# Where the expert tokens' norm weight, scale and shift are applied: on token rows or on turned blocks

## The chip, the cores and the metric

The kernel runs on one core of one Trainium2 chip. The metric is device time in microseconds (us); the kernel before was run three times with a median of 1957.68 us (1955.96 to 1957.83). TensorE does matmuls and transposes (a transpose is a matmul with an identity), VectorE and ScalarE the elementwise work, GpSimd indirect DMAs and small work, SyncE issues the weight loads. Each engine works through its own instructions in program order and waits on semaphores for the others.

## The reference, cut to what matters

The program is a transformer block with a mixture of experts, and a second block behind it. The part that the change touches, with one batch row, 1024 tokens of 1024 channels, 16 experts of 128 tokens each:

```python
x = x + ga1 * branch_merge(px, h_mx, w_fourier, w_mlstm, w_out)
hx2 = modulate(rmsnorm(x, g_norm2), sh2, sc2)       # x * rstd * g * (1 + sc2) + sh2
# expert_choice(hx2, ...)
aff  = softmax(hx2 @ w_router)                      # 1024 x 16
vals, idx = top_k(aff.T, 128)                       # each expert takes 128 tokens
xs   = hx2[idx]                                     # 16 x 128 x 1024
hid  = silu(xs @ w_gate[e]) * (xs @ w_up[e])
y    = (hid @ w_down[e]) * vals
x = x + ga2 * zeros.at[idx].add(y)
```

Products are done to float32 accuracy: each operand is split into a high and a low part, and three matmuls (high·high, high·low, low·high) stand for one.

## The kernel before, in words

`mods` holds the modulation rows in device memory: row 0 is ga1, row 1 sh2, row 2 the norm weight times (1 + sc2), called A2, row 3 ga2. `router` loads rows 2 and 1 a second time as columns, one number per partition and block of 128 channels, into `ash`.

*Output projection and router* (`out_proj`, L1397). Eight tiles of 128 tokens. While TensorE does tile t+1, lanes of small steps that a planner deals out by its own costs do the norm, the routing (`route`, L1521) and the sort of tile t. `route` computes the affinities `aff`, and turns x into the modulated row h2 = x·rstd·A2 + sh2: for tiles 0 to 6 with two VectorE operations over 128x1024, for tile 7 with one on ScalarE and two on GpSimd (L1554 on). h2 and its affinities go to device memory as `h2d`. The sort of the affinities (`top`, `join`) runs on VectorE: maxima by eights of each pair of tiles, and many small merge steps (`tk`). Behind the loop the memory product of the second block (`memory`, L1480; a key and a value half, buffers `memr`, `kvm`) is taken half by half where `next(self.mem)` stands.

*Experts* (`experts`, L1626). From the sorted lists a count matrix `cm` is built; `index(e)` gets the 128 token numbers of an expert with two matmuls, and `gather(e)` fetches their rows from `h2d` into `xs`. `transp` turns four blocks of 128x128 into one PSUM bank `pa`: ScalarE copies it, rounded, into the high half of `xT`, and VectorE subtracts that from the bank into the low half. `prod` is one product: eight steps k, each of six matmuls, with weights split by ScalarE (high) and VectorE (low) from `raw` into `w` ahead of use (`prefetch`). A transposition for a later product is put in behind steps 2 and 4 (`turned`). The order per expert: the up product of expert e, in which expert e+1's rows are turned; g·pu on VectorE (in place, in the spare columns of `xs`); the gate product of expert e+1, in which g is turned into `hT`; the down product of expert e; the weighting and the scatter-add. In the code as traced all instructions carry the line of a recording helper, L67; the names of the tiles tell them apart.

In `experts` before the first expert, the order is: two gathers, the value half of `memory`, the first splits (`prefetch`), then the turning of expert 0's rows.

Of the kernel before, what the change touches and what calls it, by code (L numbers as in the profile page):

```python
# [9 lines left out]
FT = mybir.dt.float32  # L10
# [3 lines left out]
AF = mybir.ActivationFunctionType  # L14
OP = mybir.AluOpType
# [10 lines left out]
NE = 16  # L26
# [126 lines left out]
class Kern:  # L153
# [1235 lines left out]
    def load_rows(self):  # L1389
        nc = self.nc  # L1390
        self.rr = r1, r2 = self.slot(FT, "r1"), self.slot(FT, "r2")
        self.rows = ga1, A2, sh2 = r1.t[:, 0:1024], r1.t[:, 1024:2048], r2.t[:, 0:1024]
        self.AT = r2.t[0:48, 1024:2048]
        for i, v in ((0, ga1), (2, A2), (1, sh2)):
            nc.scalar.dma_start(v, self.bcast(self.mods[i:i + 1], 1024))

    def out_proj(self):  # L1397

# [102 lines left out]
    def post(self, n, ps, x, h2, hT, t):  # L1501

        nc = self.nc
        sm = self.sm[:, (t % 2) * 32:(t % 2) * 32 + 32]
        c = slice(n * 512, (n + 1) * 512)
        self.soon(ps)
        nc.vector.tensor_mul(h2[:, c], ps, self.rows[0][:, c])
        nc.vector.tensor_add(x[:, c], x[:, c], h2[:, c])
        nc.scalar.activation(h2[:, c], x[:, c], AF.Square, accum_out=sm[:, n:n + 1])
        yield  # L1510
        yield 1.0
        yield from self.until(x[:, c])
        p = self.bank("pa", (4, 128))
        for k in range(4):
            nc.tensor.transpose(p[:, k], x[:, (4 * n + k) * 128:(4 * n + k + 1) * 128], self.idn)
        nc.scalar.activation(hT[:, 4 * n:4 * n + 4], p, AF.Copy)
        yield 0.6
        if n:
            self.spawn(self.route(t, x, h2, hT), 2)

    def route(self, t, x, h2, hT):  # L1521

        nc = self.nc
        g = nc.gpsimd
        sm = self.sm[:, (t % 2) * 32:(t % 2) * 32 + 32]
        _, A2, sh2 = self.rows
        nc.sync.dma_start(self.x1d[t * 128:(t + 1) * 128], x)
        yield 0.6
        yield from self.until(hT)
        p = self.bank("pa")  # L1530
        for k in range(8):
            nc.tensor.matmul(p[0:16, 0:128], self.wr[:, k], hT[:, k], start=(k == 0), stop=(k == 7))
        lg = self.tk.t[0:16, 1920:2048]
        if t < 7:
            nc.scalar.activation(lg, p[0:16, 0:128], AF.Copy)
        else:
            self.soon(p[0:16, 0:128])
            nc.vector.tensor_copy(lg, p[0:16, 0:128])
        g.tensor_add(sm[:, 2:3], sm[:, 0:1], sm[:, 1:2])
        self.inv_sqrt(sm[:, 3:4], sm[:, 2:3], 1.0 / D, EPS)  # L1540
        yield 0.6
        yield from self.until(lg)
        p = self.bank("pa")
        nc.tensor.transpose(p[:, 0:16], lg, self.idn[0:16, 0:16])
        z = sm[:, 8:24]
        self.soon(p[:, 0:16], sm[:, 3:4])
        nc.vector.scalar_tensor_tensor(z, p[:, 0:16], sm[:, 3:4], self.shw, op0=OP.mult, op1=OP.add)
        nc.vector.tensor_reduce(sm[:, 4:5], z, axis=AX.X, op=OP.max, negate=True)
        nc.scalar.activation(z, z, AF.Exp, bias=sm[:, 4:5], accum_out=sm[:, 5:6])
        self.soon(sm[:, 5:6])  # L1550
        nc.vector.reciprocal(sm[:, 5:6], sm[:, 5:6])
        nc.vector.tensor_scalar(self.aff[:, :, 0:16], z[:, None, :].to_broadcast([128, 2, 16]), sm[:, 5:6], None,
                                op0=OP.mult)
        if t < 7:  # L1554
            nc.vector.scalar_tensor_tensor(h2[:, 0:1024], x, sm[:, 3:4], A2, op0=OP.mult, op1=OP.mult)
            nc.vector.tensor_add(h2[:, 0:1024], h2[:, 0:1024], sh2)
        else:
            nc.scalar.activation(h2[:, 0:1024], x, AF.Copy, scale=sm[:, 3:4])
            g.tensor_mul(h2[:, 0:1024], h2[:, 0:1024], A2)
            g.tensor_add(h2[:, 0:1024], h2[:, 0:1024], sh2)  # L1560
        g.tensor_copy(h2[:, 1024:1040], self.aff[:, 0, 0:16])
        g.dma_start(self.h2d[t * 128:(t + 1) * 128], h2)
        yield 0.6
        yield from self.until(self.aff)
        p = self.bank("pa")
        nc.tensor.transpose(p[0:64, 0:128], self.aff.rearrange("p a b -> p (a b)"), self.idn)
        nc.scalar.activation(self.AT[:, t * 128:(t + 1) * 128], p[0:48, 0:128], AF.Copy)

        w = self.tk.t[0:48]
        at = 768 + 128 * (t // 2) if t < 6 else 1536  # L1570
        new = w[:, 1408:1536]
        q = 32 * (t % 2)
        nc.scalar.activation(w[q:q + 16, at:at + 128], p[q:q + 16, 0:128], AF.Copy)
        if t % 2:
            self.spawn(self.top(w[:, at:at + 128], w[:, 1280:1408] if t == 1 else new, 0), 1)
            if t > 1:
                self.spawn(self.join(new), 1)
        self.routed += 1
        yield 0.5
# [46 lines left out]
    def experts(self, r2):  # L1626
        nc = self.nc
# [26 lines left out]
        xs = {}  # L1654
# [17 lines left out]
                                         in_offset=bass.IndirectOffsetOnAxis(ap=self.idx[:, e:e + 1], axis=0))  # L1672
            xs[e] = s

        def transp(src, o, k4):

            hi, lo = (o.t[:, i * 1024:(i + 1) * 1024] for i in range(2))
            p = self.bank("pa", (4, 128))
            for k in range(4):
                kk = k4 * 4 + k  # L1680
                nc.tensor.transpose(p[:, k], src[:, kk * 128:(kk + 1) * 128], self.idn)
            pf = p.rearrange("p a b -> p (a b)")
            c = slice(k4 * 512, (k4 + 1) * 512)
            nc.scalar.activation(hi[:, c], pf, AF.Copy)
            nc.vector.tensor_sub(lo[:, c], pf, hi[:, c].bitcast(FT))

        def prod(o, between=None):

# [9 lines left out]
                    between(k)  # L1698
            return pss

        def turned(src, dst, key):

            def between(k):
                if k == 2:
                    dst[key] = self.slot(FR, "xT")
                if k in (2, 4):
                    transp(src, dst[key], k // 2 - 1)
            return between

        def silu(e, pss):  # L1710
            s = xs[e].t[:, 1040:2064]
            for n in range(2):
                nc.scalar.activation(s[:, n * 512:(n + 1) * 512], pss[n], AF.Silu)
            return s

        for e in range(2):
            index(e)
            gather(e)
        next(self.mem)
        self.spare, self.ahead = 4, 3  # L1720
        self.prefetch()
        for _ in self.mem:
            pass
        xT, hT = {0: self.slot(FR, "xT")}, {}
        for k4 in range(2):
            transp(xs[0].t, xT[0], k4)
        index(2)
        self.spare, self.ahead, self.raw_max = 1, 5, 20
        self.prefetch()
# [3 lines left out]
        for e in range(NE):  # L1733
            if e == NE - 1:
# [1 line left out]
                nc.gpsimd.dma_start(ir.t[:, 0:1024], self.bcast(self.I["iota"], 1024))  # L1736
                nc.gpsimd.tensor_scalar(io.t[:, 0:1024], ir.t[:, 0:1024], self.last, None, op0=OP.is_equal)
                self.free(ir)
            pu = prod(xT[e], turned(xs[e + 1].t, xT, e + 1) if e + 1 < NE else None)
            self.free(xT.pop(e))  # L1740
            for n in range(2):
                c = slice(n * 512, (n + 1) * 512)
# [1 line left out]
            if e + 1 < NE:  # L1744
                if e + 2 < NE:
                    gather(e + 2)
                g[e + 1] = silu(e + 1, prod(xT[e + 1], turned(g[e], hT, e)))
            if e == NE - 1:
                hT[e] = self.slot(FR, "xT")
                for k4 in range(2):  # L1750
# [572 lines left out]
```

## Time and profile before

| quantity | value |
|---|---|
| median of 3 runs | 1957.68 us (1955.96 to 1957.83) |
| profiled execution, its own time | 1955.41 us |
| its span | 1953.6 us |
| TensorE, busy | 1871.4 us |
| VectorE, busy | 1417.4 us |
| ScalarE, busy | 872.1 us |
| GpSimd, busy | 161.2 us |
| granted TensorE clock, mean | 0.985 |

The profile comes from one execution; its span is the stretch that the hardware profiler covers, and the time of the execution is 1.8 us more. Busy time of an engine says nothing on whether it is waited for: that is read from timelines and from the waits of a stage. The granted clock is in parts of TensorE's full speed. The experts take about a third of the span.

### The profile page before, as it was taken

What the parts mean: (1) busy time and instruction counts of PE and PEld (TensorE: products, weight loads), DVE (VectorE), ACT (ScalarE), POOL (GpSimd) and SP (SyncE); (2) the same over time, 40 slices, a digit from 0 to 9 for tenths busy, and PEclk for the clock granted to TensorE, in tenths of its full rate; (3) what the DMA queues carried; (4) which work ended last, traced back from release to release, by engine and by line L of the source; (5) the groups of instructions that cost most, each with busy time, mean ns of one, the idle gap of its engine ahead of it and who ended that gap; (6) DMA issues with size and microseconds to landing.
All of it is one profiled execution on the core that took longest, in us unless ns stands there. A gap on an engine that the chain in (4) does not pass through costs nothing.

```text
span 1953.6 us, 23920 instructions
## 1 busy us (share of the span) xinstructions
PE 1871.4 (96%) x9226; PEld 1511.7 (77%) x9226; DVE 1417.4 (73%) x2129; ACT 872.1 (45%) x1243; POOL 161.2 (8%) x162
## 2 busy tenths in 40 slices
PE   6899999999999999959999999999989999999997
PEld 3687888888877787748888888888868977678786
DVE  7797675555653645689999999999973977663554
ACT  6623432322322332227777777777854223342300
POOL 1300000000000002110111001010030000000011
PEclk9999999999999999979999999999999999999999
DMA  8100125433313533478999999999951110011312
GB/s 354 65 27 14 54 87 216 172 142 130 119 69 148 173 129 135 166 311 314 378 381 381 382 395 395 400 392 387 365 183 43 34 43 22 28 45 44 129 65 76
DMA packets 64541, 361.02 MB, mean 185 GB/s; under 512 B 9742, under 2 KB 10775, under 8 KB 30380
## 3 DMA queue, kind: packets, MB, share of 16 engines
q1 hardware_dynamic: 50652, 319.22, 42.1%
q0 software_dynamic: 9680, 34.37, 5.7%
q10 hardware_dynamic: 4096, 5.91, 0.9%
q8 instruction: 72, 1.18, 0.2%
q14 instruction: 41, 0.34, 0.0%
HBM read 329.96 MB, written 29.52 MB: 184 GB/s over the span
## 4 chain that ended last, share of the span: by engine, by line
PE 89%; DVE 6%; ACT 2%; DMA 1%; issue 1%; POOL 0%; ACTq 0%; POOLq 0%; DVEq 0%; SPq 0%
PE pm L67 78%; PE pa L67 11%; DVE tk L67 1%; DVE gt L67 1%; DVE w L67 1%; DMA bd<-gd 1%; DVE mw L67 0%; DMA b<-yd 0%; DMA wgr<-in_w_g 0%; DVE tm L67 0%; ACT gt L67 0%; ACT x L67 0%; DVE b L67 0%; ACT w L67 0%; POOL stat L67 0%
## 5 line engine op out<-in xcount | busy, mean ns | idle before, releaser
L67 DVE TENSOR_TENSOR w<-raw,w 128x1024 fp32r<-128x1024 f32 (+1 forms) x500 | 586.9, 1217 | 89.6 <-ACT w L67 85.2
L67 PE MATMUL pm<-w,xT 128*128 128x512 f32 x2304 | 552.7, 397 | 3.0 <-ACT xT L67 2.5
L67 ACT ACTIVATE w<-raw 128x1024 fp32r<-128x1024 f32 (+1 forms) x500 | 507.5, 1052 | 104.9 <-PE pm L67 101.0
L67 PEld LDWEIGHTS pm<-w,xT 128*128 128x128 f32 x2304 | 429.9, 189 | 99.1 <-ACT xT L67 3.1
L67 PE MATMUL pm<-hT,w 128*128 128x512 f32 x1536 | 383.1, 401 | 0.0
L67 PEld LDWEIGHTS pm<-hT,w 128*128 128x128 f32 x1536 | 284.0, 190 | 60.5 <-issue 1.7
L67 PE MATMUL pm<-x,w 128*128 128x512 f32 x1152 | 281.1, 399 | 0.0
L67 PEld LDWEIGHTS pm<-x,w 128*128 128x128 f32 x1152 | 214.0, 188 | 54.0 <-issue 8.4
L67 PE MATMUL pm<-w,hh 128*128 128x512 f32 x480 | 111.9, 394 | 0.9 <-DVE w L67 0.9
L67 PEld LDWEIGHTS pm<-w,hh 128*128 128x128 f32 x480 | 90.1, 188 | 22.6 <-DVE w L67 1.3
L67 PE MATMUL pm<-w,mg 128*128 128x512 f32 x384 | 98.2, 403 | 0.0
L67 PEld LDWEIGHTS pm<-w,mg 128*128 128x128 f32 x384 | 69.3, 188 | 15.8 <-issue 1.5
L67 POOL DMA_INDIRECT x1d<-xs,idx x16 | 48.8, 3049 | 390.3 <-DVE xs L67 383.5
L67 DVE SCALAR_TENSOR_TENSOR qk<-raw,cols,qk 128x945 f32<-128x945 f32 (+2 forms) x64 | 78.0, 1219 | 1.3
L67 DVE SCALAR_TENSOR_TENSOR dg<-da,cols,dg 128x1023 f32<-128x1023 f32 (+29 forms) x60 | 76.1, 1268 | 1.6
L67 ACT ACTIVATE xT<-pa 128x512 fp32r<-128x512 f32 x64 | 37.6, 589 | 28.8 <-PE pa L67 26.5
L67 ACT ACTIVATE b<-pm 128x512 f32<-128x512 f32 x32 | 19.1, 598 | 66.3 <-PE pm L67 63.5
L67 PEld LDWEIGHTS pm<-w,hT 128*128 128x128 f32 x384 | 46.0, 189 | 2.2 <-ACT w L67 0.9
L67 PE MATMUL pm<-w,hT 128*128 128x256 f32 x384 | 46.8, 283 | 0.2 <-DVE w L67 0.2
L67 PE MATMUL pm<-om,w 128*128 128x512 f32 x192 | 45.2, 395 | 1.7 <-ACT om L67 0.9
L67 PEld LDWEIGHTS pm<-w,x 128*128 128x128 f32 x384 | 45.7, 189 | 0.1
L67 PE MATMUL pm<-w,x 128*128 128x256 f32 x384 | 45.8, 281 | 0.0
(364 smaller groups left out, 1961.6 us busy)
## 6 DMA issues: line engine op xcount, KB each, us to landing
raw<-in_w_gate SPq DMA_DIRECT2D x64, 1024.0 KB, 8.2
raw<-in_w_up SPq DMA_DIRECT2D x64, 1024.0 KB, 12.5
raw<-in_w_down SPq DMA_DIRECT2D x64, 1024.0 KB, 6.7
raw<-in_w_in SPq DMA_DIRECT2D x34, 1024.0 KB, 5.0
raw<-in_w_ada_rest SPq DMA_DIRECT2D x16, 1024.0 KB, 6.5
raw<-in_w_out SPq DMA_DIRECT2D x9, 1024.0 KB, 4.8
raw<-in_w_ada SPq DMA_DIRECT2D x8, 1024.0 KB, 12.5
b<-yd SPq DMA_DIRECT2D x16, 512.0 KB, 3.9
```

The lines of the kernel that those rows point to most:

```text
L67: return f(*a, **kw)
```

## The change

Rows are gathered as x·rstd only. A2 and sh2 are applied after the turning, where a channel is a partition, as scale and bias operands (`ash`) of the ScalarE copy. As such an operand is one number per partition, each 128x128 block needs an activation of its own, and the full value is written twice: rounded into `xT` (high) and unrounded into spare columns of `xs` (`tmp`), from which VectorE makes the low part. `turned` takes a function; the turning of g stays as it was. The broadcast loads of A2 and sh2 go. `next(self.mem)` ahead of the first `prefetch` goes: the value half is now taken by the loop behind it, after the first splits.

```diff
     def load_rows(self):
-        self.rows = ga1, A2, sh2 = r1.t[:, 0:1024], r1.t[:, 1024:2048], r2.t[:, 0:1024]
+        self.ga1 = r1.t[:, 0:1024]
-        for i, v in ((0, ga1), (2, A2), (1, sh2)):
-            nc.scalar.dma_start(v, self.bcast(self.mods[i:i + 1], 1024))
+        nc.scalar.dma_start(self.ga1, self.bcast(self.mods[0:1], 1024))
...
     def route(self, t, x, h2, hT):
-        if t < 7:
-            nc.vector.scalar_tensor_tensor(h2[:, 0:1024], x, sm[:, 3:4], A2, op0=OP.mult, op1=OP.mult)
-            nc.vector.tensor_add(h2[:, 0:1024], h2[:, 0:1024], sh2)
-        else:
-            nc.scalar.activation(h2[:, 0:1024], x, AF.Copy, scale=sm[:, 3:4])
-            g.tensor_mul(h2[:, 0:1024], h2[:, 0:1024], A2)
-            g.tensor_add(h2[:, 0:1024], h2[:, 0:1024], sh2)
+        nc.scalar.activation(h2[:, 0:1024], x, AF.Copy, scale=sm[:, 3:4])
...
-        def transp(src, o, k4):
+        def transp(src, o, k4, tmp=None):
...
-            nc.scalar.activation(hi[:, c], pf, AF.Copy)
-            nc.vector.tensor_sub(lo[:, c], pf, hi[:, c].bitcast(FT))
+            if tmp is None:
+                nc.scalar.activation(hi[:, c], pf, AF.Copy)
+                nc.vector.tensor_sub(lo[:, c], pf, hi[:, c].bitcast(FT))
+                return
+            for out, at in ((hi, k4 * 512), (tmp, 0)):
+                for k in range(4):
+                    kk = k4 * 4 + k
+                    nc.scalar.activation(out[:, at + k * 128:at + (k + 1) * 128], p[:, k], AF.Identity,
+                                         scale=self.ash[:, 0, kk:kk + 1], bias=self.ash[:, 1, kk:kk + 1])
+            nc.vector.tensor_sub(lo[:, c], tmp, hi[:, c].bitcast(FT))
...
+        def rows(e, o, k4):
+
+            transp(xs[e].t, o, k4, xs[e].t[:, 1040:1552])
...
         for e in range(2):
             index(e)
             gather(e)
-        next(self.mem)
         self.spare, self.ahead = 4, 3
         self.prefetch()
         for _ in self.mem:
             pass
         xT, hT = {0: self.slot(FR, "xT")}, {}
         for k4 in range(2):
-            transp(xs[0].t, xT[0], k4)
+            rows(0, xT[0], k4)
...
-            pu = prod(xT[e], turned(xs[e + 1].t, xT, e + 1) if e + 1 < NE else None)
+            pu = prod(xT[e], turned(lambda o, k4: rows(e + 1, o, k4), xT, e + 1) if e + 1 < NE else None)
...
-                g[e + 1] = silu(e + 1, prod(xT[e + 1], turned(g[e], hT, e)))
+                g[e + 1] = silu(e + 1, prod(xT[e + 1], turned(lambda o, k4: transp(g[e], o, k4), hT, e)))
```

VectorE's order at the end of the output projection, before: the last tile's softmax (`sm`, `aff`), then merge steps of the sort (`tk`), then the maxima of the last pair of tiles.

```order
RECIPROCAL sm<-sm 128x1
TENSOR_SCALAR aff<-sm 128x2x16
TENSOR_TENSOR tk_5352<-tk_5352 48x4x16 x2
TENSOR_TENSOR tk_5352<-tk_5352 48x8x8 x2
TENSOR_TENSOR tk_5352<-tk_5352 48x16x4 x2
TENSOR_TENSOR tk_5352<-tk_5352 48x32x2 x2
TENSOR_TENSOR tk_5352<-tk_5352 48x64 x2
TENSOR_TENSOR tk_5352<-tk_5352 48x128
TENSOR_TENSOR tk_5352<-tk_5352 48x64 x2
TENSOR_TENSOR tk_5352<-tk_5352 48x2x32 x2
```

The same place on VectorE now:

```order
SCALAR_TENSOR_TENSOR sm<-pa_6308,sm,shw 128x16
TENSOR_REDUCE sm<-sm 128x1
RECIPROCAL sm<-sm 128x1
TENSOR_SCALAR aff<-sm 128x2x16
MAX tk_5350<-tk_5350 48x8 x2
MATCH_REPLACE tk_5350<-tk_5350 48x64 x2
```

Before, 25 merge steps stand between `aff` and the first maxima; now they stand ahead of the softmax of the last tile.

ScalarE's order at the start of the experts, before: copies of the key half and the value half (`kvm`), the first splits (`w`), expert 0's turned rows (`xT`).

```order
ACTIVATE kvm_6308<-pm_6309 128x256
ACTIVATE kvm_6308<-pm_6319 128x256
DMA ga_637_6425<-mods 128x1024
ACTIVATE kvm_6308<-pm_6445 128x256
ACTIVATE kvm_6308<-pm_6455 128x256
ACTIVATE w_6471<-raw_6214 128x1024
ACTIVATE w_6474<-raw_6214 128x1024
ACTIVATE w_6477<-raw_6219 128x1024
ACTIVATE xT_6484<-pa_6485 128x512
ACTIVATE xT_6484<-pa_6492 128x512
```

The same place on ScalarE now:

```order
ACTIVATE w_6434<-raw_6229 128x1024
ACTIVATE w_6437<-raw_6229 128x1024
ACTIVATE w_6440<-raw_6236 128x1024
ACTIVATE kvm_6322<-pm_6449 128x256
ACTIVATE kvm_6322<-pm_6459 128x256
ACTIVATE xT_6471<-pa_6472,ash 128x128 x4
ACTIVATE xs_6423<-pa_6472,ash 128x128 x4
ACTIVATE xT_6471<-pa_6486,ash 128x128 x4
ACTIVATE xs_6423<-pa_6486,ash 128x128 x4
```

The three splits moved ahead of the value half's copies, and each turned block is eight activations in place of one.

ScalarE's order in an up product, before, with weight splits around the two turned blocks of the next expert:

```order
ACTIVATE w_6921<-raw_6678 128x1024
ACTIVATE xT_6932<-pa_6933 128x512
ACTIVATE w_6946<-raw_6704 128x1024
ACTIVATE w_6955<-raw_6704 128x1024
ACTIVATE xT_6932<-pa_6958 128x512
```

And now:

```order
ACTIVATE w_6938<-raw_6695 128x1024
ACTIVATE xT_6949<-pa_6950,ash 128x128 x4
ACTIVATE xs_6714<-pa_6950,ash 128x128 x4
ACTIVATE w_6970<-raw_6721 128x1024
ACTIVATE w_6979<-raw_6721 128x1024
ACTIVATE xT_6949<-pa_6982,ash 128x128 x4
ACTIVATE xs_6714<-pa_6982,ash 128x128 x4
```

The places among the splits are the same; what stands in them is longer. VectorE's order behind it now, with the low parts of rows and weights and the multiplication g·pu (`xs<-xs,pm`), which has the same place as before:

```order
TENSOR_TENSOR xT_6949<-xs_6714,xT_6949 128x512
TENSOR_TENSOR w_6970<-raw_6721,w_6970 128x1024
TENSOR_TENSOR w_6979<-raw_6721,w_6979 128x1024
TENSOR_TENSOR xT_6949<-xs_6714,xT_6949 128x512
TENSOR_TENSOR w_6996<-raw_6741,w_6996 128x1024
TENSOR_TENSOR w_7005<-raw_6741,w_7005 128x1024
TENSOR_TENSOR w_7016<-raw_6794,w_7016 128x1024
TENSOR_TENSOR xs_6432<-xs_6432,pm_6912 128x512
TENSOR_TENSOR xs_6432<-xs_6432,pm_6913 128x512
```

The low parts of the rows read `xs` (the unrounded copy) where they read the PSUM bank `pa` before.

## Rows read from the trace of the kernel before

**Rows 1.** The page: engine, busy us, share of the span, instructions.

```profile
PE 1871.4 (96%) x9226; PEld 1511.7 (77%) x9226; DVE 1417.4 (73%) x2129; ACT 872.1 (45%) x1243; POOL 161.2 (8%) x162
```

**Rows 2.** Windows: us, PE, PEld, DVE, ACT, POOL busy, PEclk, DMA share, GB/s.

```profile
760.00:800.00 40.00, 39.98 (x200) 30.61 (x198) 26.93 (x102) 10.38 (x32) 7.75 (x14) 1.00 0.37 139
832.30:858.60 26.30, 7.18 (x33) 6.04 (x34) 24.91 (x109) 1.82 (x5) 6.42 (x5) 0.74 0.90 372
910.00:1380.00 470.00, 470.00 (x2147) 384.18 (x2146) 451.52 (x490) 362.55 (x400) 50.24 (x26) 1.00 1.01 387
```

**Rows 3.** Timeline into the experts: start, us, engine, operation, count [idle before <-releaser].

```profile
832.27 9.15 DVE L67 TENSOR_TENSOR tk<-tk 48x64 f32<-48x64 f32 x25
...
833.11 0.27 ACT L67 ACTIVATE tk<-pa 16x128 f32<-16x128 f32 x1
...
841.34 0.34 DVE L67 MAX8 tk<-tk 48x8 f32<-48x64 f32 x2
...
860.47 7.72 PE L67 MATMUL pm<-raw,memr 128*128 128x256 f32 x32
...
861.88 1.06 POOL L67 DMA_INDIRECT xs<-h2d,idx  x1 [22.08 <-DVE ga L67]
...
868.23 0.39 ACT L67 ACTIVATE kvm<-pm 128x256 f32<-128x256 f32 x1 [3.07 <-PE pm L67]
868.51 2.94 ACT L67 ACTIVATE w<-raw 128x1024 fp32r<-128x1024 f32 x3
...
871.35 1.07 ACT L67 ACTIVATE xT<-pa 128x512 fp32r<-128x512 f32 x2
...
873.74 17.42 PE L67 MATMUL pm<-w,xT 128*128 128x512 f32 x64 [0.54 <-DVE xT L67]
```

**Rows 4.** DMA issues, median us to landing: first gather, then those of 900:1380.

```profile
xs<-h2d,idx POOLq DMA_INDIRECT x1, 4.3
...
xs<-h2d,idx POOLq DMA_INDIRECT x13, 9.4
```

**Rows 5.** Small activations: pairs in the timeline, then groups by form (busy, mean ns).

```profile
325.11 0.45 ACT L67 ACTIVATE va<-pm 128x128 f32<-128x128 f32 x2 [5.35 <-PE pm L67]
...
396.43 0.63 ACT L67 ACTIVATE ml<-pa,rcol 128x128 f32<-128x128 f32 x2 [8.69 <-DVE rcol L67]
...
L67 ACT ACTIVATE hT<-pa,shx,sx 128x512 fp32r<-128x512 f32 x16 | 11.9, 777 | 3.6 <-PE pa L67 3.5
...
L67 ACT ACTIVATE x<-pa,cols 128x512 fp32r<-128x512 f32 x16 | 10.4, 689 | 5.4 <-PE pa L67 5.3
...
L67 ACT ACTIVATE ml<-pa,rcol 128x128 f32<-128x128 f32 x32 | 10.0, 364 | 40.9 <-DVE rcol L67 40.9
...
L67 ACT ACTIVATE va<-pm 128x128 f32<-128x128 f32 x32 | 7.1, 275 | 41.9 <-PE pm L67 41.9
```

**Rows 6.** Windows around the start of the first product.

```profile
871.00:872.00 1.00, 0.02 (x1) 0.02 (x1) 1.00 (x2) 1.00 (x3) 0.00 (x0) 1.00 1.00 426
872.00:873.00 1.00, 1.00 (x2) 0.48 (x2) 1.00 (x1) 1.00 (x2) 0.00 (x0) 0.51 1.01 418
```

**Rows 7.** Timeline of a steady expert: up product, then the turning of g.

```profile
963.36 0.60 ACT L67 ACTIVATE xT<-pa 128x512 fp32r<-128x512 f32 x1 [0.78 <-PE pa L67]
964.75 1.06 ACT L67 ACTIVATE w<-raw 128x1024 fp32r<-128x1024 f32 x1 [0.79 <-PE pm L67]
...
966.15 1.06 ACT L67 ACTIVATE w<-raw 128x1024 fp32r<-128x1024 f32 x1 [0.34 <-PE pm L67]
...
967.11 0.58 ACT L67 ACTIVATE xT<-pa 128x512 fp32r<-128x512 f32 x1
...
968.98 3.49 DVE L67 TENSOR_TENSOR w<-raw,w 128x1024 fp32r<-128x1024 f32 x3
...
972.39 1.28 DVE L67 TENSOR_TENSOR xs<-xs,pm 128x512 f32<-128x512 f32 x2
...
974.67 0.60 PE L67 MATMUL pa<-kc,xs 128*128 128x128 f32 x4
```

More of the change, by code (lines that the diff above doesn't have):

```diff
@@ L1506, in post @@
         self.soon(ps)
-        nc.vector.tensor_mul(h2[:, c], ps, self.rows[0][:, c])
+        nc.vector.tensor_mul(h2[:, c], ps, self.ga1[:, c])
         nc.vector.tensor_add(x[:, c], x[:, c], h2[:, c])
@@ L1525, in route @@
         sm = self.sm[:, (t % 2) * 32:(t % 2) * 32 + 32]
-        _, A2, sh2 = self.rows
         nc.sync.dma_start(self.x1d[t * 128:(t + 1) * 128], x)
@@ L1699, in prod, with turned @@
             return pss
-        def turned(src, dst, key):
+        def rows(e, o, k4):
+            transp(xs[e].t, o, k4, xs[e].t[:, 1040:1552])
+        def turned(f, dst, key):
             def between(k):
@@ L1706, in between @@
                 if k in (2, 4):
-                    transp(src, dst[key], k // 2 - 1)
+                    f(dst[key], k // 2 - 1)
             return between
```

## The prediction, made before the changed kernel ran

> **What bounds the kernel now.** I first read the page's busy shares [rows 1]. TensorE is busy 96% of the span, VectorE 73%, ScalarE 45%: only time in which TensorE stands still, or runs at its lower clock, can be won or lost. The busy time by stretches [rows 2] says where. In the output projection (760 to 800) TensorE has no gap in 40 us, with VectorE busy 26.93 and ScalarE 10.38. Between 832.3 and 858.6 it works 7.18 of 26.30 us: this is the tail of the router, and VectorE, 24.91 busy, sets its end. From 910 to 1380 TensorE is busy all 470.00, VectorE 451.52 (96%), ScalarE 362.55 (77%): thirteen experts with no gap at all. So two places count: the hole ahead of the experts, and whether the experts stay without gaps.
>
> **The hole.** Its timeline [rows 3]: VectorE runs 25 small merge steps of the sort from 832.27, and only at 841.34 begins the top-8 chain of the last two tiles. From there to the first gather (861.88) everything hangs in one chain: maxima, index matmuls, gather. TensorE then does the value product (860.47, 7.72 us) and turns expert 0's rows. ScalarE does the last copy of the value product at 868.23, three weight splits from 868.51, and from 871.35 the turned rows; expert 0's gate product runs without a break from 873.74.
>
> *Sort.* Seven tiles lose two 128x1024 operations each on VectorE, at about 1.16 (3.49 for three in [rows 7]) some 16 us, beside a TensorE without gaps; directly that is worth nothing. But the 25 merge steps fit into that room: in the order of the changed kernel the maxima stand right behind the last tile's `aff` (the first two pieces of the order shown with the change). The chain starts when the last tile's lists are copied, 833.11 + 0.27 = 833.4, in place of 841.34: −7.9 us. Bounds: 0, if the last copies come later for another reason, and −9.1, the 25 steps whole. I take −7.9. The added ScalarE work (seven copies at 0.98, from 2.94 for three) has 30 of 40 us idle to lie in; without that room it would be 7 us. That the two broadcast loads and the last tile's two GpSimd operations go is worth nothing: the chain of maxima does not read what they write, and the rows' write to memory, which they precede, has until the first gather.
>
> *Gather.* 7.9 us earlier the first gather is issued at 854.0. It landed in 4.3 us in its place before, while thirteen later ones, among weight loads, took 9.4 in the median [rows 4]. The value product now lies from about 852.6 to 860.3; a landing at 854.0 + 4.3 = 858.3 is hidden, one at 854.0 + 9.4 = 863.4 is 3.1 late. The queue is as full in the hole (share 0.90) as where the 4.3 was measured; I take +0.5, with bounds 0 and +3.3.
>
> *First product.* The first three splits now stand ahead of the value copies, so ScalarE comes to the turned rows at 868.6, behind the value copy (868.23 + 0.39), instead of 871.35, on the time axis of the trace of before: 2.7 earlier. But a turned block is eight small activations now and not one. Their price: rows of 128x128 from PSUM take 275 ns without a pointer operand, and a pair of them 0.45, so each after the first adds 0.175; with one pointer (`rcol`) they take 364, a pair 0.63, so 0.27 each [rows 5]. A second pointer costs 777 − 689 = 88 ns (`hT` against `x`, both 128x512), so 0.357 each is my estimate for scale and bias; a block is 8 × 0.357 = 2.86 us against 0.60 for the copy, 2.26 more. The low part comes only behind the second four. The first block is there at 868.6 + 2.86 = 871.5, its low part 0.6 to 0.8 later, so matmuls without a break start at 872.3 rather than 873.74: 1.4 earlier. The fourth split stands behind both blocks: 868.6 + 5.72 + 0.98 = 875.3 on ScalarE, its low part 1.2 later, 876.5; ahead of its use lie 18 matmuls, at least 18 × 17.42 / 64 = 4.9 us, so to 877.2, and it is not late. TensorE's granted clock fell in this hole: 1.00 in 871 to 872, then 0.51 in 872 to 873 [rows 6] (0.51 is the lower level, 1.2 GHz; TensorE had been busy 0.02 of the 1.00 us before). I leave that as it is: between −0.6, if the low clock simply begins later, and −2.2 I take −1.2. Sum of the start: −7.9 + 0.5 − 1.2 = −8.6.
>
> **The experts.** This is where the change costs. A steady up product [rows 7]: TensorE turns the next expert's rows in two blocks, ScalarE copies each in about 0.60 (963.36 and 967.11), and weight splits stand between and behind. VectorE, in program order, does three low parts from 968.98 (3.49) and then at 972.39 the multiplication g·pu; its first half (1.28 for two) ends at 973.03. The gate product's turning of g at 974.67 needs it: margin 1.6 us. The pattern repeats in experts 1 to 14.
>
> Now put 2.26 in twice. ScalarE's first block starts as before at 963.36 and ends 966.22. The two splits behind it, 0.96 each when nothing holds them (966.15 to 967.11), end at 968.1, where they ended 967.11 before: 1.25 of the 2.26 goes into the waits that stood before those splits (0.79 and 0.34, for `w` buffers that TensorE frees). The second block ends 968.1 + 2.86 = 971.0, the next split 971.9, and behind it VectorE's three low parts run from about 972.0 to 975.5, 3.1 later than before. They cannot move back: VectorE takes 3.49 for three where ScalarE takes 2.94. g·pu starts at 975.5, its first half is there at 976.13, and TensorE, ready at 974.67, stands still for 1.5 us. Queued behind that turning are all matmuls of the gate product, since TensorE works in order; nothing catches this up, as it has no gap in which to. Nor do the weights: a stall that TensorE takes in every expert gives ScalarE the same time back, so the stall repeats and does not grow.
>
> Up products that turn rows: fifteen (experts 0 to 14). Fourteen at 1.5 = 21.0. The first comes with little lead: the splits begin with the product instead of running ahead, so I take 2.0 (bounds 0 and 4.5, both blocks in full). Sum +23.0.
>
> The bounds of the price: at 0.175 per activation (no pointer) a block is 1.4 us, and the stall is 2 × 8 × (0.357 − 0.175) = 2.9 smaller, so none. The stall is zero up to 0.264 each. The upper end is the duration alone, 0.364 + 0.088 = 0.45 without overlap: 3.0 us of stall, +44 for fifteen. Nearest the operation asked for is the pair's rate with its pointer added, so 0.357.
>
> The Trainium skill ("ScalarE: Activation LUTs", What ACT_TABLE_LOAD costs) gives 186 ns plus 0.833 ns per element, about 93 more for each pointer operand and an overlap of about 93 between neighbours. For 128 elements and two pointers this would be an estimate of 0.386 each, against my 0.357. Its 93 agrees with the 88 of the trace; its base does not quite: 186 + 107 = 293 where the row shows 275. By the page of the Trainium skill the stall would be near 2.0 per expert and its sum 30; the rows decide here.
>
> **Sum.** −8.6 + 23.0 = +14.4 us. The profiled execution took 1955.41 (span 1953.6 and 1.8 around it): 1969.8. The median of the runs, 1957.68, is 2.3 above it, so the forecast is 1972, with an own range of 1960 to 1982.
>
> **Rivals.**
> 1. *The margin carries it* (the other side). If neighbouring small activations overlap better than the pairs show, at or below 0.264 each, VectorE is at most 1.6 late and TensorE never waits. For it: ScalarE is only 77% busy and the pair's 0.175 lies far below. Against: 16 activations need 2.26 × 2 more, and one-pointer pairs already show 0.27. Then only the start counts: 1957.7 − 8.6, with about 2 lost in the first expert: 1949 to 1951. The point that decides is 0.264 for a stall and about 0.30 for the whole (a stall of 0.58 × 15 eats up the start). Chance 0.12.
> 2. *Half of it* (0.30 to 0.31 each): stall 0.6, fifteen times 9, against −8.6: no change, 1957 to 1958. Chance 0.08.
> 3. *A dearer activation.* A pair overlaps by 2 × 0.364 − 0.63 = 0.10; if two pointers halve that, an activation costs 0.40, the stall is 16 × (0.40 − 0.264) = 2.2, fifteen times 33, less 8.6: +24, about 1982; with 0.38, 1978. For it: the whole length of 0.45 is worked out from measured ones, and no row shows an overlap with two pointers. Against: the overlap is the same 0.10 with none (2 × 0.275 − 0.45) and with one. Chance 0.12. By the Trainium skill ("ScalarE: Activation LUTs", the section above) this would be the likeliest case.
> 4. *A late gather* lies in the forecast's own range: landing 9.4 after issue, the start is worth 8.6 − 2.8 = 5.8, so 1957.7 + 23 − 5.8 = 1975.
>
> Chance of the forecast 0.68.
>
> **How the numbers follow.** About 0.2% (3.9 us) is what a measurement of this kernel can tell from no change. Faster by more: rival 1, less its slower tail, 0.11. Within: rival 2 and a remainder, 0.09. Slower: forecast and rival 3, 0.80. The range 1956 to 1983 takes in the forecast, rival 2's upper part and rival 3; left out are rival 1 and the dearest activations.
>
> **What would show it.** The changed profile should have: the maxima right behind `aff` at about 833.4 and the first gather at about 854; the turned rows as groups of four 128x128 activations with 0.357 a piece; in every gate product an idle TensorE of about 1.5 us ahead of the turning of g, released by VectorE's multiplication in `xs`; a steady expert longer by that much. The forecast is wrong if TensorE keeps 470 of 470 busy, if the small activations come at 0.27 or less, or if the wait stands elsewhere: at a weight's low part, which would mean that ScalarE and not VectorE's order ends last.

## The result, and the profile after

The changed kernel took 1971.81 us in the median (1968.69 to 1973.41, 4 runs), the kernel before 1957.22 in the same count: a ratio of 1.0073, with a 95% interval of 1.006 to 1.0086. It is slower by 14.6 us; 1972 was forecast. The profiled execution has a span of 1968.7 us.

The windows of the changed kernel that answer to [rows 2] (us, busy time of PE, PEld, DVE, ACT, POOL, then PEclk, DMA share, GB/s):

```profile
760.00:800.00 40.00, 39.99 (x206) 31.02 (x206) 20.67 (x101) 12.73 (x34) 4.37 (x12) 1.00 0.37 133
832.30:858.60 26.30, 13.82 (x53) 11.53 (x54) 22.83 (x100) 5.58 (x10) 4.15 (x5) 0.74 1.01 421
910.00:1380.00 470.00, 454.03 (x2064) 368.35 (x2063) 433.21 (x474) 398.07 (x562) 47.19 (x26) 1.00 0.99 372
```

In the output projection VectorE lost 6 of 27 us and TensorE is as full as before: no direct gain. In the hole TensorE works 6.6 us more, since the index matmuls and the value product, which stand ahead of the experts, now fall into this window. In the experts it now stands still for 16 of 470 us. The waits of that stretch name the place (who waited for whom: us, times, longest):

```profile
PEld pa L67 <- DVE xs L67: 21.6, 13, 1.7
PE pa L67 <- DVE xs L67: 16.0, 13, 1.3
```

Thirteen waits of 1.23 us, all of a turning (`pa`) for VectorE's g·pu (`xs`), one per expert. The steady expert's timeline, the answer to [rows 7]:

```profile
960.32 1.50 ACT L67 ACTIVATE xT<-pa,ash 128x128 fp32r<-128x128 f32 x4 [0.75 <-PE pa L67]
961.70 1.52 ACT L67 ACTIVATE xs<-pa,ash 128x128 f32<-128x128 f32 x4
...
964.97 1.54 ACT L67 ACTIVATE xT<-pa,ash 128x128 fp32r<-128x128 f32 x4
966.34 1.56 ACT L67 ACTIVATE xs<-pa,ash 128x128 f32<-128x128 f32 x4
...
968.88 3.50 DVE L67 TENSOR_TENSOR w<-raw,w 128x1024 fp32r<-128x1024 f32 x3 [0.22 <-ACT w L67]
...
972.29 1.28 DVE L67 TENSOR_TENSOR xs<-xs,pm 128x512 f32<-128x512 f32 x2
...
973.03 0.66 PE L67 MATMUL pa<-kc,xs 128*128 128x128 f32 x4 [1.20 <-DVE xs L67]
```

A block of eight takes 2.75 us (960.32 to 963.07, where the weight splits go on), so 0.343 per activation. VectorE's three low parts and the multiplication are back to back as before; they only start later, 8.56 us behind the first block's start (968.88 − 960.32) where it was 5.62 (968.98 − 963.36 in [rows 7]), and TensorE has been waiting 1.20 us when the first half is there.

The start of the experts, the answer to [rows 3]:

```profile
833.42 0.24 DVE L67 TENSOR_SCALAR aff<-sm 128x32 f32<-128x32 f32 x1
...
834.71 0.35 DVE L67 MAX8 tk<-tk 48x8 f32<-48x64 f32 x2 [1.04 <-ACT tk L67]
...
853.80 8.60 PE L67 MATMUL pm<-raw,memr 128*128 128x256 f32 x32
...
855.22 1.07 POOL L67 DMA_INDIRECT xs<-h2d,idx  x1 [18.86 <-DVE ga L67]
...
863.90 1.07 PE L67 MATMUL pa<-kc,xs 128*128 128x128 f32 x8 [1.50 <-DMA xs<-h2d,idx]
...
868.25 4.16 PE L67 MATMUL pm<-w,xT 128*128 128x512 f32 x17 [2.34 <-DVE xT L67]
...
873.75 11.14 PE L67 MATMUL pm<-w,xT 128*128 128x512 f32 x47 [1.34 <-DVE w L67]
```

The maxima follow the affinities directly. These times can't be set against those of before as they stand: this execution was already 1.8 us later when the output projection began, a part that the change does not touch. The first fence here is of before, the second of the changed kernel; the second row of each is the first matmul behind the last expert:

```profile
711.94 0.63 PE L67 MATMUL pm<-w,mg 128*128 128x512 f32 x2
...
1443.00 0.47 PE L67 MATMUL pa<-yl,io 128*128 128x512 f32 x1 [0.89 <-ACT yl L67]
```

```profile
713.70 0.40 PE L67 MATMUL pm<-w,mg 128*128 128x512 f32 x1
...
1459.11 0.47 PE L67 MATMUL pa<-yl,io 128*128 128x512 f32 x1 [0.90 <-ACT yl L67]
```

So the table counts from that matmul, for every kernel of this document; each entry is a difference of two starts in its own trace (the steady expert from the start of expert 1's down product to that of expert 2's). An entry comes from one profiled execution, a median from all runs of its kernel.

| kernel | first gather | expert 0's turning | expert 0's up product | a steady expert | median us |
|---|---|---|---|---|---|
| before | 149.95 | 156.09 | 174.89 | 35.92 | 1957.22 |
| changed | 141.51 | 150.20 | 166.86 | 37.40 | 1971.81 |
| one copy (e1) | 141.53 | 150.29 | 163.01 | 36.01 | 1944.43 |
| one pointer (e2) | 141.51 | 149.95 | 165.17 | 36.01 | 1948.19 |
| turn at 4, 6 (e3) | 141.55 | 150.02 | 166.67 | 36.15 | 1953.42 |
| value half first (e4) | 141.54 | 149.46 | 167.42 | 37.32 | 1974.0 |
| old router tail (e5) | 149.88 | 157.02 | 173.67 | 37.42 | 1977.87 |
| turn at 3, 5 (e6) | 141.55 | 150.33 | 167.00 | 35.88 | 1953.34 |
| turn at 4, 6, quick start (e7) | 141.55 | 150.23 | 165.39 | 36.16 | 1952.52 |
| before, turn at 4, 6 (e8) | 149.82 | 155.92 | 174.70 | 36.00 | 1959.22 |
| GpSimd rows (e9) | 141.95 | 148.57 | 167.63 | 39.10 | 1980.9 |
| turn at 3, 5, quick start (e10) | 141.60 | 150.74 | 165.88 | 36.06 | 1952.73 |
| GpSimd rows, quick start (e11) | 141.83 | 148.18 | 164.81 | 39.09 | 1976.96 |
| round the copy (e12) | 141.58 | 150.84 | 165.54 | 35.98 | 1947.79 |

The medians belong to runs of before that lie between 1956.5 and 1957.6.

### The profile page after: what moved, and what is told of

Read it like the earlier page. It is cut to its first block, busy times and chain, and to the rows that moved or that the text cites. A ratio compares the mean times of both kernels' runs of the same rounds, so it can differ in the third digit from the quotient of the medians.

```text
span 1968.7 us, 24123 instructions
## 1 busy us (share of the span) xinstructions
PE 1873.4 (95%) x9226; PEld 1512.0 (77%) x9226; DVE 1394.5 (71%) x2115; ACT 943.9 (48%) x1474; POOL 146.0 (7%) x160
## 4 chain that ended last, share of the span: by engine, by line
PE 68%; DVE 14%; DMA 8%; ACT 5%; issue 4%; POOL 0%; ACTq 0%; POOLq 0%; DVEq 0%; SPq 0%
PE pm L67 59%; PE pa L67 10%; DVE w L67 7%; DMA raw<-in_w_up 5%; DVE xs L67 1%; ACT w L67 1%; ACT xs L67 1%; DVE gt L67 1%; ACT xT L67 1%; DMA raw<-in_w_down 1%; DVE ga L67 1%; DVE tk L67 1%; DMA bd<-gd 1%; DMA raw<-in_w_gate 1%; DVE mw L67 0%
## 5 line engine op out<-in xcount | busy, mean ns | idle before, releaser
L67 ACT ACTIVATE w<-raw 128x1024 fp32r<-128x1024 f32 (+1 forms) x500 | 501.9, 1070 | 73.6 <-PE pm L67 71.4
L67 PE MATMUL pa<-kc,xs 128*128 128x128 f32 x256 | 39.1, 276 | 20.9 <-DVE xs L67 19.4
L67 PEld LDWEIGHTS pa<-kc,xs 128*128 128x128 f32 x256 | 30.3, 140 | 34.4 <-DVE xs L67 26.5
L67 DVE TENSOR_TENSOR xT<-xs,xT 128x512 fp32r<-128x512 f32 x32 | 22.5, 702 | 46.0 <-ACT xs L67 46.0
L67 ACT ACTIVATE xT<-pa,ash 128x128 fp32r<-128x128 f32 x128 | 48.7, 480 | 12.3 <-PE pa L67 12.3
L67 ACT ACTIVATE xs<-pa,ash 128x128 f32<-128x128 f32 x128 | 49.3, 505 | 0.0
```

The costliest lines, as they stand in the source:

```text
L67: return f(*a, **kw)
```

## The experiments

**e1, one copy per block.** One 128x512 copy, no scale and no shift.

```diff
-            if tmp is None:
+            if True:
```

> The changed kernel with each turned block of rows copied by one 128x512 activation, as before; scale and shift are left out of the computation. Theory (the 16 small activations per expert push g·pu past TensorE's need of it): no stall ahead of the turning of g, steady experts back to about 36.0 and 35.0 us, and the first product earlier too; 1971.8 - 15 x 1.43 - about 1 to 3 = 1947 to 1950 us. Rival (the experts are slower because VectorE reads the rows' low parts from other places, or because weights come later): within 5 us of 1972.

Measured: 1944.43 us, ratio 0.9937 (0.9918 to 0.9955), below the range. TensorE is busy all of the 470:

```profile
910.00:1380.00 470.00, 470.00 (x2152) 384.38 (x2152) 451.09 (x487) 361.99 (x398) 50.28 (x27) 1.00 1.01 388
```

The small activations cost 27.4 us by the medians: in the traces 3.85 up to expert 0's up product (166.86 against 163.01), and 22.6 from there to the end of the experts, as stalls. What remains of the change without them is a gain of 12 us.

**e2, one pointer operand.** Still eight activations per block, the shift left out.

```diff
-                                         scale=self.ash[:, 0, kk:kk + 1], bias=self.ash[:, 1, kk:kk + 1])
+                                         scale=self.ash[:, 0, kk:kk + 1])
```

> The changed kernel with the scale operand alone on the small activations (the shift is left out of the computation), so sixteen activations per expert as in the changed kernel, but one pointer operand each. Theory with the price as the dose: 0.343 us each was seen with two pointers; with one 0.25 to 0.27, a block 2.0 to 2.1 us, at the point where the stall vanishes (0.264): stall 0 to 0.2 per expert, 1949 to 1954 us. Rival (the number of instructions counts, not the pointers): a stall of over 1 us stays, above 1965 us.

Measured: 1948.19 us, ratio 0.9962 (0.995 to 0.9974), just below the range. A block's two rows:

```profile
960.00 1.14 ACT L67 ACTIVATE xT<-pa,ash 128x128 fp32r<-128x128 f32 x4 [0.75 <-PE pa L67]
961.02 1.16 ACT L67 ACTIVATE xs<-pa,ash 128x128 f32<-128x128 f32 x4
```

Four come in 1.02 us, 0.255 each, and the stall is gone but for 0.6 us at one place and 0.7 at the last expert. So it is not the count of instructions: the same sixteen cost next to nothing 0.09 us cheaper, below the 0.264 at which the prediction put the end of the stall.

**e3, g turned later.** Steps 4 and 6 of the gate product in place of 2 and 4; `turned` takes the first step as an argument.

```diff
-                g[e + 1] = silu(e + 1, prod(xT[e + 1], turned(lambda o, k4: transp(g[e], o, k4), hT, e)))
+                g[e + 1] = silu(e + 1, prod(xT[e + 1], turned(lambda o, k4: transp(g[e], o, k4), hT, e, 4)))
```

> The changed kernel with the two turnings of g behind steps 4 and 6 of the gate product in place of 2 and 4, nothing else. Theory (TensorE waits only because it needs g·pu 2.8 us too early): no idle ahead of the turning of g, steady experts 36.0 and 35.0 us, 1971.8 - 15 x 1.43 = about 1950 us (1948 to 1953). Rival (ScalarE and VectorE cannot keep the pace, the lead of the weights shrinks expert by expert): the stall comes back as waits for a weight's low part, 1965 us or more.

Measured: 1953.42 us, ratio 0.9977 (0.9968 to 0.9987), a little above the range. g·pu and the turning in this kernel:

```profile
971.71 1.28 DVE L67 TENSOR_TENSOR xs<-xs,pm 128x512 f32<-128x512 f32 x2
...
973.87 0.60 PE L67 MATMUL pa<-kc,xs 128*128 128x128 f32 x4
```

Nothing waits, though ScalarE does all the work of the changed kernel: the stall was one of order, not of throughput. The missing 3 us stand in two places. Of the 20.1 us that experts 1 to 14 had lost, 18.4 come back; the weight load ahead of the down product now waits 0.3 for the low part of g, 15 times (first row, 900 to 1430), and what is left is 1.7. And at the last expert, whose g is turned by itself behind its up product, TensorE waits 2.1 us for g·pu (second row, its only wait over 0.15 us in that stretch): from expert 14's down product to expert 15's it takes 25.96, in the changed kernel 24.44, before 23.87.

```profile
PEld pm L67 <- DVE xT L67: 4.4, 15, 0.5
PE pa L67 <- DVE xs L67: 2.1, 1, 2.1
```

This last wait comes back in every run that turns g later on the changed kernel (e6, e7 and e10: 2.2 to 2.3).

**e4, the value half first.** As in the kernel before, ahead of the first splits.

```diff
             gather(e)
+        next(self.mem)
         self.spare, self.ahead = 4, 3
```

> The changed kernel with the value half of the memory product taken ahead of the first splits again, as before the change. Theory (of the start, the earlier sort chain carries nearly all and the earlier splits about 1 us): 1972 to 1974 us, the first gather at the same place, expert 0's turned rows on ScalarE 2 to 3 us later. Rival (the splits carry the start): 1976 us or more.

Measured: 1974.0 us, ratio 1.0087 (1.007 to 1.0104). Expert 0's up product starts 0.56 later than in the changed kernel: that much of the start is the splits' place, in one trace each.

**e5, the old router tail.** The lines that the change removed from `load_rows` and `route` stand again.

```diff
-        nc.scalar.activation(h2[:, 0:1024], x, AF.Copy, scale=sm[:, 3:4])
+        if t < 7:
+            nc.vector.scalar_tensor_tensor(h2[:, 0:1024], x, sm[:, 3:4], A2, op0=OP.mult, op1=OP.mult)
+            nc.vector.tensor_add(h2[:, 0:1024], h2[:, 0:1024], sh2)
...
```

> The changed kernel with the router's old tail: norm weight, scale and shift applied to the token rows again (two VectorE operations per tile, two on GpSimd for the last), with their broadcast loads; the turned rows then get scale and shift a second time, so the computation is that of other numbers. Theory (the earlier start comes from the 25 merge steps that fit into the room those operations leave): the merge steps stand behind the last tile's affinities again, the first gather 8.4 us later, 1971.8 + 8.4 = 1980 us (1978 to 1982). Rival (the start comes from the splits ahead of the value half): 1972 to 1974 us.

Measured: 1977.87 us, ratio 1.0112 (1.0095 to 1.0129), just below the range. The merge steps are back between affinities and maxima, and the first gather is 8.37 us later:

```profile
833.03 0.24 DVE L67 TENSOR_SCALAR aff<-sm 128x32 f32<-128x32 f32 x1
833.18 9.14 DVE L67 TENSOR_TENSOR tk<-tk 48x64 f32<-48x64 f32 x25
...
842.25 0.34 DVE L67 MAX8 tk<-tk 48x8 f32<-48x64 f32 x2
```

The up product comes 6.81 later, not 8.37: the turning follows the gather 7.14 behind, where the changed kernel needs 8.69.

**e6, g turned at steps 3 and 5.** As e3, one step instead of two.

```diff
-... transp(g[e], o, k4), hT, e, 4)
+... transp(g[e], o, k4), hT, e, 3)
```

> The changed kernel with g turned behind steps 3 and 5 of the gate product, one step (1.4 us) later than in the changed kernel. Theory (margin): the stall of 1.43 us per expert shrinks to 0 to 0.1, and turning two steps later has already bought all there is: 1952 to 1955 us, like the run with steps 4 and 6. Rival (something else than the distance was mended by moving two steps): half of the gain, about 1962 us.

Measured: 1953.34 us, ratio 0.9988 (0.9978 to 0.9997). One step of 1.4 us takes the whole stall of experts 1 to 14, as a margin short by 1.2 to 1.4 should; half of it did not stay.

**e7, later turning and a quick start.** For expert 0 VectorE makes the unrounded copy; four splits ahead.

```diff
+                    if dve and out is tmp:
+                        nc.vector.tensor_scalar(out[:, at + k * 128:at + (k + 1) * 128], p[:, k],
+                                                self.ash[:, 0, kk:kk + 1], self.ash[:, 1, kk:kk + 1], op0=OP.mult, op1=OP.add)
+                        continue
...
-        self.spare, self.ahead = 4, 3
+        self.spare, self.ahead = 4, 4
```

> The changed kernel with g turned behind steps 4 and 6, and at the start two edits for expert 0: VectorE makes the unrounded copy of its turned rows (four tensor_scalar of 128x128 from PSUM, scale and shift in one) while ScalarE makes the rounded one, and four weight splits in place of three stand ahead of the value half's copies. Theory (of the run with one copy per block, 3.7 us of the gain at the start lie in the first product, where ScalarE does 16 small activations and the fourth split waits behind them): 2 to 3 us below the run with steps 4 and 6, 1950 to 1952 us. Rival (VectorE and ScalarE reading one PSUM bank hold each other up, or the gather is the bound): no gain, 1953 to 1955 us.

Measured: 1952.52 us, ratio 0.9981 (0.997 to 0.9991). In the trace the up product starts 1.28 earlier than in e3; the medians differ by 0.9, within their scatter, and the forecast of 2 to 3 us was too much. The rival was half right: VectorE began on the bank only behind ScalarE's four, not beside them.

```profile
862.66 2.90 ACT L67 ACTIVATE xT<-pa,ash 128x128 fp32r<-128x128 f32 x8 [1.96 <-PE pa L67]
...
864.20 1.37 DVE L67 TENSOR_SCALAR xs<-pa,ash 128x128 f32<-128x128 f32 x4 [5.69 <-ACT xT L67]
```

**e8, the kernel before with the later turning.**

```diff
-                g[e + 1] = silu(e + 1, prod(xT[e + 1], turned(g[e], hT, e)))
+                g[e + 1] = silu(e + 1, prod(xT[e + 1], turned(g[e], hT, e, 4)))
```

> The kernel before with g turned behind steps 4 and 6, nothing else. Theory (before had 1.6 us of margin and no stall, so a later turning has nothing to give): within 3 us of before, rather 0 to 3 slower, since the later low parts of g come closer to the down product (0.2 us per expert in the run on the changed kernel). Rival (turning later is a gain of its own, apart from the small activations): 1950 us or less.

Measured: 1959.22 us, ratio 1.0016 (1.0004 to 1.0028). No gain where there was no stall: what e3 gives back is the stall and not a merit of that order.

**e9, GpSimd applies scale and shift.** From expert 1 on, on the gathered rows, with one copy per block.

```diff
             xs[e] = s
+            if e:
+                v = s.t[:, 0:1024]
+                nc.gpsimd.tensor_mul(v, v, self.mrow[0])
+                nc.gpsimd.tensor_add(v, v, self.mrow[1])
...
-            transp(xs[e].t, o, k4, xs[e].t[:, 1040:1552])
+            transp(xs[e].t, o, k4, None if e else xs[e].t[:, 1040:1552])
```

> The changed kernel, but from expert 1 on GpSimd multiplies and adds the rows (two 128x1024 operations in place, right behind each gather; A2 and the shift stay in a buffer), so that a turned block is one 128x512 copy again; expert 0 keeps its 16 small activations, g is turned behind steps 2 and 4 as before. Theory (only the small activations on ScalarE stall TensorE, and GpSimd, busy 50 of 470 us, has the room): steady experts 36.0 and 35.0 us without a stall, the start as in the changed kernel: 1971.8 - 22 = 1949 to 1951 us. Rival (GpSimd's operations, 2.4 us each in the trace of before, and one buffer less slow VectorE or the loads): 1955 us or more.

Measured: 1980.9 us, ratio 1.0118 (1.0102 to 1.0133). The theory was wrong here and the rival right: GpSimd had the time, VectorE had not. While GpSimd works, VectorE's low parts take 5.71 us for three (3.49 in [rows 7]), and GpSimd itself 6.81 for its two. The third row is the last of those three by itself, 3.44; the first two took 1.22 each:

```profile
897.28 5.71 DVE L67 TENSOR_TENSOR w<-raw,w 128x1024 fp32r<-128x1024 f32 x3
898.45 6.81 POOL L67 TENSOR_TENSOR xs<-xs,r 128x1024 f32<-128x1024 f32 x2 [3.72 <-DMA xs<-h2d,idx]
...
899.55 3.44 DVE L67 TENSOR_TENSOR w<-raw,w 128x1024 fp32r<-128x1024 f32 x1
...
902.91 0.68 DVE L67 TENSOR_TENSOR xT<-pa,xT 128x512 fp32r<-128x512 f32 x1
903.51 2.83 DVE L67 TENSOR_TENSOR w<-raw,w 128x1024 fp32r<-128x1024 f32 x1
```

The window of the experts, and TensorE's waits in 900 to 1430:

```profile
910.00:1380.00 470.00, 450.46 (x2026) 360.36 (x2025) 469.05 (x466) 340.92 (x373) 173.94 (x49) 1.00 0.98 365
```

```profile
PE pa L67 <- DVE xs L67: 10.9, 10, 1.4
PE pm L67 <- DVE w L67: 9.9, 10, 1.5
```

VectorE, 469.05 of 470, became the bound; TensorE waits for it at g·pu and at weights. The kernel also holds one buffer more for the rows of scale and shift; what that costs was not run apart.

**e10, steps 3 and 5 with the quick start.** The edits of e6 and e7 together.

> The changed kernel with g turned behind steps 3 and 5 and the quick start for expert 0 (VectorE's unrounded copy, four splits ahead). Theory (both edits work apart: steps 3 and 5 lose no 0.2 us per expert at the down product, the quick start gives 1.3 us): 1950 to 1952 us. Rival (the few late multiplications seen with steps 3 and 5 eat that): 1952 to 1955 us.

Measured: 1952.73 us, ratio 0.9969 (0.9957 to 0.9981), in the rival's range. Not distinguishable from e3, e6 and e7; the wait at the last expert, 2.3, is there too.

**e11, GpSimd's rows with the quick start.** The edits of e9 and e7's start.

> GpSimd's rows from expert 1 on together with the quick start for expert 0. Theory: 1 to 2 us below the run with GpSimd's rows alone, 1947 to 1950 us, below both kernels by more than the measurement's noise. Rival (GpSimd's operations cost elsewhere): 1954 us or more.

Measured: 1976.96 us, ratio 1.0092 (1.0078 to 1.0107): e9's loss, 4 us less of it; the expectation fell with e9's.

**e12, round the copy.** Four small activations write the unrounded copy; one copy of that, without pointers, writes the rounded half. Four splits ahead as in e7.

```diff
-            for out, at in ((hi, k4 * 512), (tmp, 0)):
-                for k in range(4):
-                    kk = k4 * 4 + k
-                    nc.scalar.activation(out[:, at + k * 128:at + (k + 1) * 128], p[:, k], AF.Identity,
-                                         scale=self.ash[:, 0, kk:kk + 1], bias=self.ash[:, 1, kk:kk + 1])
+            for k in range(4):
+                kk = k4 * 4 + k
+                nc.scalar.activation(tmp[:, k * 128:(k + 1) * 128], p[:, k], AF.Identity,
+                                     scale=self.ash[:, 0, kk:kk + 1], bias=self.ash[:, 1, kk:kk + 1])
+            nc.scalar.activation(hi[:, c], tmp, AF.Copy)
```

> The changed kernel with five activations per block in place of eight: four small ones with scale and shift write the unrounded copy, and one 128x512 copy of that makes the rounded one; four splits ahead of the value half's copies. g is turned behind steps 2 and 4 as in the changed kernel, rows are in full float32 as there. Theory (ScalarE's time per block decides, stall zero up to about 2.1 us per block): a block is 4 x 0.343 + 0.5 to 0.6 = 1.9 to 2.0 us, like the run with one pointer operand; steady experts 36.0 and 35.0 us, start like that run or 1 us better: 1946 to 1950 us, below both kernels. Rival (the copy waits for the small activations' writes, or the low part comes too late): 1955 us or more.

Measured: 1947.79 us, ratio 0.9955 (0.9941 to 0.9969): 9 us below the kernel before in the same runs, 24 below the changed one, with the whole computation. The steady expert:

```profile
955.02 1.50 ACT L67 ACTIVATE xs<-pa,ash 128x128 f32<-128x128 f32 x4 [0.75 <-PE pa L67]
956.56 0.63 ACT L67 ACTIVATE xT<-xs 128x512 fp32r<-128x512 f32 x1
...
965.54 1.28 DVE L67 TENSOR_TENSOR xs<-xs,pm 128x512 f32<-128x512 f32 x2
966.27 0.43 PEld L67 LDWEIGHTS pa<-kc,xs 128*128 128x128 f32 x4 [0.20 <-DVE xs L67]
966.34 0.60 PE L67 MATMUL pa<-kc,xs 128*128 128x128 f32 x4
```

A block is 1.50 + 0.63 = 2.1 us: the multiplication comes at the last moment; the weight load waits 0.20 and the matmul shows no wait. Against e1's 1944.43 the larger part of what is left is the start, 2.5 us up to expert 0's up product. The run has two edits, and what the fourth split ahead gives by itself was not run; that the stall is gone is the work of the five activations, since the steady expert is 35.98.

## Why the prediction was right

*Sort.* Forecast −7.9; the first gather moved by 149.95 − 141.51 = 8.44, and e5 moved it back by 8.37. The other 0.5 is that the last affinities themselves came 0.46 earlier behind the start of the output projection (833.42 − 713.70, before 832.12 − 711.94). Cause and size are shown; which of the removed lines lets the planner put the merge steps earlier, e5, which brings all of them back, does not tell apart.

*Gather.* Forecast +0.5, and here the step was too small: the turning of expert 0 came only 5.9 earlier, so 2.5 of the 8.4 were lost. The gather landed 8.6 us after issue, and the turning at 863.90 waited 1.50 for it. That is near the 9.4 of the experts and not the 4.3 of [rows 4]. The reading that failed is that the queue in the hole (share 0.90) is as full as where the 4.3 was measured: 0.90 is the mean of 832.3 to 858.6, but the gather of before was under way from 861.88 to 866.2, and in the first two of these us the share was 0.53. Now it is 1.00 while the gather is under way. First fence before, second changed:

```profile
860.00:862.00 2.00, 2.00 (x7) 1.57 (x6) 1.97 (x8) 0.00 (x0) 0.12 (x1) 0.55 0.89 360
862.00:864.00 2.00, 2.00 (x11) 1.77 (x10) 0.56 (x3) 0.00 (x0) 1.70 (x2) 1.00 0.53 160
```

```profile
850.00:856.00 6.00, 4.04 (x10) 3.26 (x11) 4.87 (x13) 0.00 (x0) 0.78 (x1) 0.50 1.00 418
856.00:860.00 4.00, 4.00 (x18) 3.46 (x17) 3.34 (x3) 0.38 (x1) 1.59 (x2) 0.89 1.00 408
```

The other 0.9 is the value product, 8.60 against 7.72. In both kernels it begins at the lower clock; by the shares 0.55 and 0.89 of these rows it stayed there for an estimated 1.3 us before (from 860.47) and 3.1 now (from 853.80).

*First product.* Forecast −1.2, from the turning on it is (166.86 − 150.20) − (174.89 − 156.09) = −2.1. The matmuls without a break begin 4.35 us behind the turning (868.25 − 863.90) in place of 5.72 (873.74 − 868.02), so 1.4 earlier, as forecast. Two other parts were wrong in the forecast, and they partly cancel. The fourth split was late, by 1.34 at 873.75, where I had it in time. ScalarE had it done at about 871.0; but VectorE works the index of the third gather (`ga`) between the rows' low parts and this split's, 1.6 us that the forecast left out, and the 17 matmuls ahead took 4.16 us and not 4.9:

```profile
870.06 7.77 ACT L67 ACTIVATE w<-raw 128x1024 fp32r<-128x1024 f32 x8
870.90 0.75 DVE L67 TENSOR_SCALAR_CACHE_REDUCE ga<-pa,kc 128x512 f32<-128x512 f32 x1
...
872.47 14.86 DVE L67 TENSOR_TENSOR w<-raw,w 128x1024 fp32r<-128x1024 f32 x13
```

So the small activations cost 3.85 here (e1) where I had counted 2.26. And the clock, which I left as before, did not fall in this product (before 0.51 at the same place in [rows 6]); that is the rest, about 2.1:

```profile
866.00:868.00 2.00, 0.00 (x0) 0.00 (x0) 0.50 (x1) 2.00 (x7) 0.00 (x0) 1.00 0.55 225
872.00:874.00 2.00, 0.66 (x3) 0.26 (x2) 1.97 (x5) 2.00 (x4) 0.00 (x0) 1.00 0.00 0
```

TensorE stood still in that stretch too, 2.3 us before 868.25 and 1.3 before 873.75, and what kept the clock up these runs don't tell. It is not the change by itself: e3 has the same start, with a wait of 2.35 ahead of the product (2.34 here), and there the clock fell, as in e4 and e5; in e6 it did not. In e3 the fall cost nothing, because the slower matmuls filled the time in which the changed kernel waits for the fourth split: from the first matmul to the up product it is 15.28 in e3 (867.30 to 882.58) and 15.29 in the changed kernel (865.27 to 880.56). Of e3, a row of the timeline and a window:

```profile
870.27 16.62 PE L67 MATMUL pm<-w,xT 128*128 128x512 f32 x64 [2.35 <-DVE xT L67]
872.00:874.00 2.00, 2.00 (x6) 1.63 (x5) 1.68 (x4) 2.00 (x4) 0.00 (x0) 0.50 0.00 0
```

The start as a whole: −8.0, forecast −8.6.

*The price of an activation.* 0.357 was put together from a pair and a pointer, 0.343 was measured, 0.255 with one pointer (0.266 by the pair). The Trainium skill ("ScalarE: Activation LUTs", What ACT_TABLE_LOAD costs) gave 0.386 as an estimate; its 93 ns per pointer agrees with 0.343 − 0.255 = 0.088, its base is too high here.

*The stall.* Forecast 1.5 each, fourteen times: the experts 1 to 14 grew by 20.1 in all, 1.4 each (the steady one by 37.40 − 35.92 = 1.48), of which 1.23 is the wait itself. VectorE's low parts came 2.9 later behind the first block (8.56 − 5.62), where 3.1 was forecast. Place, releaser and cause are as forecast: e1 and e2 take it away by ScalarE's time, e3 and e6 by TensorE's need. That it repeats without growing, and that no weight is late behind the first product, holds as well. The first expert lost 1.7 in place of 2.0 (its up product's start to its down product's).

Up to the end of the experts the changed kernel is 14.35 later (from 713.70 to 1459.11, before from 711.94 to 1443.00), forecast 14.4. The mechanism of the stall was right and so was its size; that the sum is this close is luck, since its terms are further off and nearly cancel: the gather cost 2 us more; the sort and the first product gave 0.5 and 0.9 more, the stalls cost 0.9 less (20.1 for 21.0), the first expert 0.3 less, and the last expert lost 0.6 that no step foresaw (24.44 against 23.87). With 0.343 per activation none of the first three rivals' conditions held. The first one's condition was brought about by e2 and e12, and its forecast, 1949 to 1951, came out a little too high. The fourth's, the late gather, did hold, but not its 1975, as the sort and the first product gave more.

## What to carry to other kernels

Work moved to an engine that is 77% busy is not free: look for the place where its results are next due, and set the added time against that one margin (here 1.6 us against 2 × (2.75 − 0.60) = 4.3 added). A stall of order can be mended by order (turn later, which here left a new wait at the last expert) or by fewer operands (scale and shift once, then round the copy); price both before adding an engine. Before handing elementwise work to an idle GpSimd, see what VectorE does in that time.

## What the hardware showed that was not expected

GpSimd and VectorE slow one another in e9, and not evenly: while two GpSimd operations of 128x1024 ran, single 128x1024 subtractions on VectorE took 3.44 and 2.83 us (899.55 and 903.51) while another that ran beside GpSimd too (898.41) took 1.22, as it does alone. Between 880 and 1430 those that overlap a GpSimd operation took either 1.21 to 1.23 or 2.83 to 3.44, nothing between. GpSimd's operations took 3.4 each here, where a pair took 4.78 in the tail of the router before:

```profile
833.00 4.78 POOL L67 TENSOR_TENSOR tx<-tx,r 128x1024 f32<-128x1024 f32 x2 [3.32 <-ACT tx L67]
```

The Trainium skill (GPSIMD Engine Reference, Key points) says that GpSimd shares its SBUF interfaces with VectorE, with contention for VectorE's instructions of two SBUF inputs. The low parts of weights have two, and some of them take longer; in this stretch the low part of a turned block, which reads PSUM and SBUF, kept its length (0.68 in e9's trace at 902.91). That agrees with the page. The rival of e9 had named the slower VectorE, without a size.

In e7 VectorE waited for ScalarE at a PSUM bank that both only read (5.69 <-ACT xT). The Trainium skill (PSUM — Partial Sum Buffer, PSUM bank collisions raise a hardware error) tells that the compiler's scheduler adds dependencies between engines on one bank, reads too; the wait in the trace fits that, and no run here tries it otherwise.
